# Reordering the weight loads, squares, a table load and the last mean square of a one-core hybrid decoder layer

## The chip, the cores and the metric

The kernel runs on one core of one Trainium2 chip. The metric is the device time of one execution in microseconds (us); lower is better. Engines are named as in the profile: PE is TensorE (its weight loads are PEld), DVE is VectorE, ACT is ScalarE, POOL is GpSimd, SP is SyncE, which issues most transfers. The profile is one execution taken by the hardware profiler.

## What is computed

One layer of a decoder over 1024 prompt tokens and 8 x 8 sample tokens, model width 2048, in float32. The part that the change touches is the modulation, the first norm, the start of the input projection, and the last norm:

```python
mod = jax.nn.silu(c) @ w_ada + b_ada
shift, scale, gate = jnp.split(mod[:, None, :], 3, axis=-1)
xn = rmsnorm(x, norm_g) * (1.0 + scale) + shift
z = xn @ w_in
...
out = jnp.concatenate([ya, yb, yc], axis=-1) @ w_out
return x + gate * out, new_hist_a, h_last, new_hist_b, vn
...
y = rmsnorm(x, final_g)
```

Between the two projections three token mixers work on slices of `z`: a gated linear recurrence, a convolution group of width 31, and a chunked spatial gate.

## The kernel before

Activations lie with channels on the 128 partitions and tokens along the free dimension. The tokens are worked in two parts: part 0 is the first 512 prompt tokens, part 1 the other 512 and the 64 sample tokens (576 columns, in two halves of 288). Every product of the projections is made three times (`mm3`, L130 to L133): ACT rounds a weight block to a high half (`w_hi`, L97), DVE takes the remainder (`w_lo`, L98), and PE adds hi x hi, lo x hi and hi x lo.

The stage at issue is the first one. `load_x0` (L674) loads the 16 blocks of `x0`, ACT squares them, and `var_mm` sums them on PE; `rstd_rows` (L199) makes the reciprocal root, with a Sqrt on ACT that needs a table of its own; `row_bcast` spreads it to all partitions, and L727 copies it to `R0`.

The modulation needs 2048 x 4096 weights for shift and scale. They are worked in 16 units, one for each block of 128 channels. A unit is four `ada_block`s (L708): each loads 128 x 1024 weights (512 KB, `a_raw`) and issues 8 matmuls, into 32 columns of the array each, so a unit is 32 matmuls into `ps_ada`. When the unit is done, ACT copies the result (`rows`, L177), PE turns it (`ada_turn`, L181; called the turn below), DVE makes shift and scale of it (`ada_fin`, L189 to L194: the three `adam` operations), and `norm_x` makes the normed block: DVE scales x (L243), ACT writes `xn_hi` (L244), DVE writes `xn_lo` (L245).

The main loop then takes 16 steps (L732 to L738). Step i loads unit i + 1 and issues its matmuls, makes `xn[i]`, and calls `k_step(i)` (L683), which loads block i of `w_in` (128 x 768, `w_raw`), splits it, and issues 18 matmuls of 512 columns into `ps_g`. The turn of unit i + 1 is called in the middle of `k_step(i)`. After the loop, single output blocks (`ps_s`) go on, and 64 units of the gate's modulation are put between them (`gate_block`, L152: pieces of 8 matmuls).

What sets the order in each engine's queue is not the order of the code alone. The code gives each operation a priority (`tc.high_priority`), and a scheduler of the framework puts the operations of each engine in one fixed list when the kernel is built, by priorities and by its own estimate of when data are there. On the chip each engine takes its list strictly from the front.

At the end, `out_part` (L570) works part 1's last two output blocks in two halves (L622 to L659); after each half the mean square of the finished rows is summed (`rstd_of`, L654), spread with `row_bcast`, and all 16 output blocks are scaled (L657) and stored.

Of the kernel before, what the change touches and what calls it, by code (L numbers as in the profile page):

```python
# [10 lines left out]
AF = mybir.ActivationFunctionType  # L11
ALU = mybir.AluOpType
PSUM = bass.MemoryType.PSUM

P = 128
KT = 16
EPS = 1e-6
T0 = 512
# [21 lines left out]
N_GRP = 6  # L40
# [4 lines left out]
def decoder_layer(ctx: ExitStack, tc: tile.TileContext, a):  # L45
    nc = tc.nc
# [15 lines left out]
    def mi(name):  # L62
        return pmi.tile([P, 512], F32, tag="mi", name=name)
# [12 lines left out]
    ident = cpool.tile([P, P], F32, name="ident")  # L76
    make_identity(nc, ident)
    one_d = cpool.tile([P, 1], F32, name="one_d")
# [17 lines left out]
    def split(raw, hi, lo):  # L96
        nc.scalar.copy(hi, raw)  # L97
        nc.vector.tensor_tensor(lo, raw, hi.bitcast(F32), op=ALU.subtract)  # L98

    def load_w(src, n, pieces, pool=None):  # L100
        out = []
        with tc.high_priority(HP):
            raw = wp.tile([P, 1024], F32, tag="wr", name="w_raw", bufs=3)
            nc.sync.dma_start(raw[:, :n], src)
            w = n // pieces
            for q in range(pieces):
                if pool is None:
                    hi = wp.tile([P, 512], F32R, tag="wh", name="w_hi", bufs=5)
                    lo = wp.tile([P, 512], F32R, tag="wl", name="w_lo", bufs=4)
                else:  # L110
                    hi = pool.tile([P, TM], F32R, tag="t", name="w_hi")
                    lo = pool.tile([P, TM], F32R, tag="t", name="w_lo")
                split(raw[:, q * w:(q + 1) * w], hi[:, :w], lo[:, :w])
                out.append((hi, lo))
        return out
# [19 lines left out]
    with tc.high_priority(10 * HP):  # L135
        sg = ap.tile([P, KT, 9], F32, tag="sg", name="sg", bufs=1)
        nc.gpsimd.memset(cz, 0.0)
        nc.scalar.activation(sg, cT, AF.Sigmoid)
        nc.vector.tensor_tensor(sg, sg, cT, op=ALU.mult)
        nc.vector.tensor_copy(cz[:, :, 0:9], sg)  # L140

    def ada_mm(pa, raws, b, fine):
        for q in range(2):
# [36 lines left out]
    def ada_turn(pa):  # L180
        nc.tensor.transpose(pa[:, P:2 * P], rows_of["now"], ident)  # L181
        return pa[:, P:2 * P].rearrange("p (a b) -> p a b", b=32)[:, :, 0:9]

    def ada_fin(k, pa):
        pt = ada_turn(pa)
        with tc.high_priority(HP):
            dst = adam[:, 2 * k:2 * k + 2, :]
            o = VEC["b_ada"][0] + 2 * k
            nc.vector.tensor_tensor(dst, pt[:, 0:2, :],  # L189
                                    vec[:, o:o + 2].unsqueeze(2).to_broadcast([P, 2, 9]), op=ALU.add)  # L190
            nc.vector.tensor_tensor(dst, dst, pt[:, 2:4, :], op=ALU.add)
            o = VEC["norm_g"][0] + k
            sc = adam[:, 2 * k + 1, :]
            nc.vector.tensor_scalar(sc, sc, 1.0, vec[:, o:o + 1], op0=ALU.add, op1=ALU.mult)  # L194

    def halves(T):
        return [(0, 512)] if T == T0 else [(0, 288), (288, 576)]

    def rstd_rows(src, w):  # L199
        st = stp.tile([P, 3, 144], F32, tag="st", name="st", bufs=1)  # L200
        v, r, q = st[:, 0, 0:w], st[:, 1, 0:w], st[:, 2, 0:w]
        nc.vector.tensor_scalar(v, src, EPS, None, op0=ALU.add)
        nc.scalar.activation(q, v, AF.Sqrt)
        nc.vector.reciprocal(r, q)
        nc.vector.tensor_tensor(q, r, r, op=ALU.mult)
        nc.vector.tensor_tensor(q, q, v, op=ALU.mult)
        nc.vector.tensor_scalar(q, q, -0.5, 1.5, op0=ALU.mult, op1=ALU.add)
        nc.vector.tensor_tensor(r, r, q, op=ALU.mult)
        return st

    def row_bcast(st, w, j0, n):
        pb = mi("ps_bc")
        for j in range(n):
            nc.tensor.matmul(pb[:, j * w:(j + 1) * w], ident[:, 32 * (j0 + j):32 * (j0 + j) + 1].to_broadcast([P, P]),  # L214
                             st[:, 1, 0:w], start=True, stop=True)
        return pb
# [6 lines left out]
    def rstd_of(src, u, n, ones):  # L223
        pv = mi("ps_var")
        w = n // 4
        for s in src:
            var_mm(pv, s, u, w, ones, s is src[0], s is src[-1])
        return rstd_rows(pv[:, 0:w], w)
# [341 lines left out]
    def out_part(tp, T, xd, yd, mx, sizes):  # L570
# [12 lines left out]
        acc = tp.tile([P, TM], F32, tag="t", name="acc_y")  # L583
# [38 lines left out]
        if T > T0:  # L622
            fin = []
            for d in (KT - 2, KT - 1):
                x = sp_.tile([P, TM], F32, tag="xr", name="x_r")
                nc.sync.dma_start(x[:, :T], xd[d])
                ys[d] = mp.tile([P, TM], F32, tag="mx", name=f"y{d}")
                ps = pmm.tile([P, 2, 512], F32, tag="mm", name="ps_s")
                src = a["wo_s"][d - N_GRP]
                pool = tp if d < KT - 1 else None  # L630
                fin.append((d, x, ps, load_w(src[0], 1024, 2, pool) + load_w(src[1], 1024, 2, pool)))
            for (h, (u, v)) in enumerate(halves(T)):
                for (d, x, ps, hl) in fin:
                    y = ys[d]
                    g = adam[:, 32 + d, :]
                    for k in range(KT):
                        xh, xl = xs(k)
                        hi, lo = hl[k // 4]
                        o = k % 4 * P
                        mm3(ps[:, h, :v - u], hi[:, o:o + P], lo[:, o:o + P], xh[:, u:v], xl[:, u:v],  # L640
                            k == 0, k == KT - 1)
                    with tc.high_priority(HP):
                        e = min(v, T0)
                        nc.vector.scalar_tensor_tensor(y[:, u:e], ps[:, h, 0:e - u], g[:, 0:1], x[:, u:e],
                                                       op0=ALU.mult, op1=ALU.add)
                        if v > T0:
                            y3 = y[:, T0:T1].rearrange("p (b l) -> p b l", b=8)
                            nc.vector.tensor_tensor(y3, ps[:, h, T0 - u:v - u].rearrange("p (b l) -> p b l", b=8),
                                                    g[:, 1:9].unsqueeze(2).to_broadcast([P, 8, 8]), op=ALU.mult)
                            nc.vector.tensor_tensor(y[:, T0:T1], y[:, T0:T1], x[:, T0:T1], op=ALU.add)  # L650
                        nc.scalar.activation(x[:, u:v], y[:, u:v], AF.Square)
                        nc.vector.tensor_tensor(acc[:, u:v], acc[:, u:v], x[:, u:v], op=ALU.add)
                with tc.high_priority(HP):
                    pb = row_bcast(rstd_of([acc], u, v - u, one_d), (v - u) // 4, 0, 4)  # L654
                for q in range(KT):
                    yq = ys[q]
                    nc.vector.scalar_tensor_tensor(yq[:, u:v], yq[:, u:v], vs("fg", q), pb[:, :v - u],  # L657
                                                   op0=ALU.mult, op1=ALU.mult)
                    (nc.scalar if q % 2 and h else nc.sync).dma_start(yd[q][:, u:v], yq[:, u:v])  # L659
            return  # L660
# [13 lines left out]
    def load_x0(k, pv):  # L674
        with tc.high_priority(HP):
            x = mp.tile([P, TM], F32, tag="mx", name=f"x0_{k}")
            nc.sync.dma_start(x[:, :T0], a["x0"][k])
            x0.append(x)
            sq = sp_.tile([P, TM], F32, tag="xr", name="x_sq")
            nc.scalar.activation(sq[:, :T0], x[:, :T0], AF.Square)  # L680
            var_mm(pv, sq, 0, P, one_d, k == 0, k == KT - 1)

    def k_step(k, turn):  # L683
        hl = load_w(a["wi_g"][k], N_GRP * P, 2)
        xh, xl = xn[k]
        for c in range(N_GRP):
            hi, lo = hl[c // 3]
            o = c % 3 * P
            mm_unit(gt[c // 2], c % 2, hi[:, o:o + P], lo[:, o:o + P],
                    xh, xl, T0, k == 0, k == KT - 1)  # L690
            if c == 2 and turn:
                turn()

    ada_ps = {}
# [35 lines left out]
    gt.extend(pmm.tile([P, 2, 512], F32, tag="mm", name="ps_g") for _ in range(3))  # L730
    ada_fin(0, ada_ps[0])
    for i in range(KT):  # L732
        if i + 1 < KT:
            for b in range(4):
                ada_block(i + 1, b)
        with tc.high_priority(HP):
            xn[i] = norm_x(i, x0[i], R0, T0)
        k_step(i, (lambda: ada_fin(i + 1, ada_ps[i + 1])) if i + 1 < KT else None)  # L738
    loc = [(gt[c // 2], c % 2) for c in range(N_GRP)]
    nc.sync.dma_start(bs, a["bs"])  # L740
    nc.sync.dma_start(vec[:, 64:], a["vec"][:, 64:])
# [159 lines left out]
```

## Time and profile before

| | us |
|---|---|
| median of three runs | 1527.75 (1524.29 to 1527.92) |
| the profiled execution | 1527.3 |
| its span in the trace | 1525.6 |
| PE busy | 1480.7 (97%) |
| DVE busy | 931.0 (61%) |
| ACT busy | 600.9 (39%) |
| POOL busy | 47.8 (3%) |

The span is what the trace covers; 1.7 us of the profiled execution lie around it. Busy time is the time in which an engine has at least one instruction under way. PE's matmuls are pipelined, so that a matmul that the trace shows with 0.39 us starts 0.23 us after the one before it: the pitch from start to start is what counts, not the duration.

### The profile page before, as it was taken

How to read it: one execution, taken by the hardware profiler on the slowest of the kernel's cores; microseconds unless marked ns; L12 is line 12 of the kernel's file. 1: busy time of each engine (PE TensorE's matmuls, PEld its weight loads, DVE VectorE, ACT ScalarE, POOL GpSimd, SP SyncE). 2: the span in 40 equal slices, each digit the busy share in tenths (PEclk: the TensorE clock that was granted, in tenths of full speed). 3: DMA queues.
4: the chain of work that ended last, by engine and by line, in shares of the span. 5: the costliest groups of instructions: out<-in, count | busy, mean ns of one | idle time of the engine just before them, and what ended most of it. 6: DMA issues, size and time to landing. Idle time of an engine off the chain costs nothing.

```text
span 1525.6 us, 25535 instructions
## 1 busy us (share of the span) xinstructions
PE 1480.7 (97%) x10184; PEld 1316.9 (86%) x10184; DVE 931.0 (61%) x1777; ACT 600.9 (39%) x1014; POOL 47.8 (3%) x120
## 2 busy tenths in 40 slices
PE   6999999999999999999999999999999999999996
PEld 4666788888777778888899999999999999999995
DVE  2334995498657443454895996277966754334345
ACT  4224432263547443343543422225445743322220
POOL 0000000010000000000000000010000000000000
PEclk8999999999999999999999999999999999999998
DMA  9987323333444443465473222222322222243323
GB/s 360 396 287 250 98 76 97 97 91 127 166 160 149 162 161 103 139 208 171 145 247 113 75 84 90 83 75 86 101 74 83 69 74 63 79 132 123 107 78 124
DMA packets 86550, 206.10 MB, mean 135 GB/s; under 512 B 10784, under 2 KB 26656, under 8 KB 86432
## 3 DMA queue, kind: packets, MB, share of 16 engines
q1 hardware_dynamic: 85136, 203.23, 40.6%
q8 instruction: 79, 1.29, 0.3%
q10 hardware_dynamic: 1296, 1.25, 0.3%
q14 instruction: 39, 0.32, 0.1%
HBM read 194.70 MB, written 9.74 MB: 134 GB/s over the span
## 4 chain that ended last, share of the span: by engine, by line
PE 89%; DVE 5%; DMA 3%; issue 1%; ACT 1%; SPq 0%; DVEq 0%; ACTq 0%
PE ps_s L131 22%; PE ps_s L132 22%; PE ps_s L133 22%; PE ps_g L133 6%; PE ps_g L132 5%; PE ps_g L131 5%; PE ps_ada L147 3%; DMA a_raw<-w_ada 1%; DVE w_lo L98 1%; DMA x<-x 1%; PE ps_bc L214 1%; PE ps_gate L131 1%; PE ps_gate L132 0%; DMA vec<-vec 0%; DMA w_raw<-wi_g 0%
## 5 line engine op out<-in xcount | busy, mean ns | idle before, releaser
L98 DVE TENSOR_TENSOR w_lo<-w_raw,w_hi 128x512 fp32r<-128x512 f32 (+1 forms) x480 | 311.7, 653 | 408.1 <-PE ps_s L133 269.3
L131 PE MATMUL ps_s<-xn_hi,w_hi 128*128 128x288 f32 (+1 forms) x1632 | 538.3, 330 | 1.9 <-ACT pad_a L439 1.7
L97 ACT CAST w_hi<-w_raw 128x512 fp32r<-128x512 f32 (+1 forms) x480 | 281.7, 591 | 653.4 <-PE ps_s L132 462.5
L132 PE MATMUL ps_s<-xn_lo,w_hi 128*128 128x288 f32 (+1 forms) x1632 | 534.7, 328 | 0.0
L133 PE MATMUL ps_s<-xn_hi,w_lo 128*128 128x288 f32 (+1 forms) x1632 | 532.8, 326 | 0.0
L131 PEld LDWEIGHTS ps_s<-xn_hi,w_hi 128*128 128x128 f32 x1632 | 306.1, 188 | 28.8 <-issue 2.8
L133 PEld LDWEIGHTS ps_s<-xn_hi,w_lo 128*128 128x128 f32 x1632 | 307.2, 188 | 22.2 <-issue 0.4
L132 PEld LDWEIGHTS ps_s<-xn_lo,w_hi 128*128 128x128 f32 x1632 | 306.5, 188 | 21.4 <-issue 0.9
L376 DVE SCALAR_TENSOR_TENSOR mx<-pad_b,vec,mx 128x512 f32<-128x512 f32 x240 | 178.0, 746 | 2.3
L131 PE MATMUL ps_s<-m_hi,w_hi 128*128 128x288 f32 (+1 forms) x480 | 157.2, 327 | 0.0
L132 PE MATMUL ps_s<-m_lo,w_hi 128*128 128x288 f32 (+1 forms) x480 | 156.6, 326 | 0.0
L133 PE MATMUL ps_s<-m_hi,w_lo 128*128 128x288 f32 (+1 forms) x480 | 156.5, 326 | 0.0
L133 PE MATMUL ps_g<-xn_hi,w_lo 128*128 128x288 f32 (+1 forms) x288 | 95.6, 332 | 2.3 <-DVE w_lo L98 2.2
L131 PE MATMUL ps_g<-xn_hi,w_hi 128*128 128x288 f32 (+1 forms) x288 | 96.3, 334 | 1.2
L131 PEld LDWEIGHTS ps_s<-m_hi,w_hi 128*128 128x128 f32 x480 | 90.0, 188 | 6.5 <-issue 0.2
L133 PEld LDWEIGHTS ps_s<-m_hi,w_lo 128*128 128x128 f32 x480 | 90.3, 188 | 6.1
L132 PEld LDWEIGHTS ps_s<-m_lo,w_hi 128*128 128x128 f32 x480 | 90.1, 188 | 6.3
L131 PE MATMUL ps_g<-m_hi,w_hi 128*128 128x288 f32 (+1 forms) x288 | 94.2, 328 | 0.1
L132 PE MATMUL ps_g<-xn_lo,w_hi 128*128 128x288 f32 (+1 forms) x288 | 94.3, 327 | 0.0
L132 PE MATMUL ps_g<-m_lo,w_hi 128*128 128x288 f32 (+1 forms) x288 | 93.9, 326 | 0.0
L133 PE MATMUL ps_g<-m_hi,w_lo 128*128 128x288 f32 (+1 forms) x288 | 93.6, 326 | 0.0
L133 PEld LDWEIGHTS ps_g<-xn_hi,w_lo 128*128 128x128 f32 x288 | 54.2, 188 | 12.3 <-DVE w_lo L98 8.9
(199 smaller groups left out, 1475.2 us busy)
## 6 DMA issues: line engine op xcount, KB each, us to landing
w_raw<-wi_s SPq DMA_DIRECT2D x136, 512.0 KB, 3.6
w_raw<-wo_s SPq DMA_DIRECT2D x40, 512.0 KB, 3.5
a_raw<-w_ada SPq DMA_DIRECT2D x64, 256.0 KB, 6.9
a_raw<-w_ada SPq DMA_DIRECT2D x32, 512.0 KB, 7.4
g_raw<-w_ada SPq DMA_DIRECT2D x64, 256.0 KB, 3.1
w_raw<-wi_g SPq DMA_DIRECT2D x16, 384.0 KB, 7.1
w_raw<-wo_g SPq DMA_DIRECT2D x16, 384.0 KB, 3.0
w_raw<-wi_g SPq DMA_DIRECT2D x32, 192.0 KB, 2.4
```

The source lines that it names most:

```text
L97: nc.scalar.copy(hi, raw)
L98: nc.vector.tensor_tensor(lo, raw, hi.bitcast(F32), op=ALU.subtract)
L131: nc.tensor.matmul(out, wh, xh, start=start, stop=False)
L132: nc.tensor.matmul(out, wh, xl, start=False, stop=False)
L133: nc.tensor.matmul(out, wl, xh, start=False, stop=stop)
L147: nc.tensor.matmul(pa[32 * j:32 * j + 32, 0:P], cz[:, k, :], raws[q][:, j * P:(j + 1) * P], start=(t == 0), stop=(t == (7 if fine else 15)))
L214: nc.tensor.matmul(pb[:, j * w:(j + 1) * w], ident[:, 32 * (j0 + j):32 * (j0 + j) + 1].to_broadcast([P, P]), st[:, 1, 0:w], start=True, st ...
L376: nc.vector.scalar_tensor_tensor(out[:, :T0], pad[:, j:j + T0], w[:, j:j + 1], out[:, :T0], op0=ALU.mult, op1=ALU.add)
```

## The change

Four edits:

1. The load and the split of block i of `w_in` move from the head of `k_step` to the head of the loop's step, ahead of the loads of unit i + 1.
2. A Sqrt of one column is put behind the Sigmoid at the very start, so that the root's table is loaded there.
3. Of the 16 squares of `x0`, the eight of odd k go to DVE.
4. The mean square of the last two half stages is not summed by four matmuls into 32 partitions each, with tokens along the free dimension, but by three matmuls of one column each, with 96 tokens on the partitions: the root is then worked on a tile of 96 x 3 instead of 128 x 72, and three matmuls of 96 columns spread it.

```diff
         nc.vector.tensor_copy(cz[:, :, 0:9], sg)
+        nc.scalar.activation(sg[:, 0, 0:1], one_d, AF.Sqrt)
...
-    def rstd_rows(src, w):
+    def rstd_rows(src, w, p=P):
         st = stp.tile([P, 3, 144], F32, tag="st", name="st", bufs=1)
-        v, r, q = st[:, 0, 0:w], st[:, 1, 0:w], st[:, 2, 0:w]
+        v, r, q = st[0:p, 0, 0:w], st[0:p, 1, 0:w], st[0:p, 2, 0:w]
...
-                    pb = row_bcast(rstd_of([acc], u, v - u, one_d), (v - u) // 4, 0, 4)
+                    pv, pb = mi("ps_var"), mi("ps_bc")
+                    w = 96
+                    for c in range((v - u) // w):
+                        nc.tensor.matmul(pv[0:w, c:c + 1], acc[:, u + c * w:u + (c + 1) * w], one_d,
+                                         start=True, stop=True)
+                    st = rstd_rows(pv[0:w, 0:(v - u) // w], (v - u) // w, w)
+                    for c in range((v - u) // w):
+                        nc.tensor.matmul(pb[:, c * w:(c + 1) * w], st[0:w, 1, c:c + 1].to_broadcast([w, P]),
+                                         ident[0:w, 0:w], start=True, stop=True)
...
-            nc.scalar.activation(sq[:, :T0], x[:, :T0], AF.Square)
+            if k % 2:
+                nc.vector.tensor_tensor(sq[:, :T0], x[:, :T0], x[:, :T0], op=ALU.mult)
+            else:
+                nc.scalar.activation(sq[:, :T0], x[:, :T0], AF.Square)
...
-    def k_step(k, turn):
-        hl = load_w(a["wi_g"][k], N_GRP * P, 2)
+    def k_step(k, hl, turn):
...
     for i in range(KT):
+        hl = load_w(a["wi_g"][i], N_GRP * P, 2)
         if i + 1 < KT:
             for b in range(4):
                 ada_block(i + 1, b)
         with tc.high_priority(HP):
             xn[i] = norm_x(i, x0[i], R0, T0)
-        k_step(i, (lambda: ada_fin(i + 1, ada_ps[i + 1])) if i + 1 < KT else None)
+        k_step(i, hl, (lambda: ada_fin(i + 1, ada_ps[i + 1])) if i + 1 < KT else None)
```

Because the scheduler lays the lists anew, the first edit changes the lists of PE, DVE and ACT in the main loop as well, not only SP's.

PE in the main loop before, the same in every step: from the end of one step's product through the whole of the next unit and its turn into the next step (`ps_ada<-a_raw` are a unit's matmuls, `ps_ada<-ident,rows` is the turn, `ps_g` the product).

```order
L133 MATMUL ps_g<-xn_hi,w_lo 128x512
L147 MATMUL ps_ada<-a_raw,cz 32x128 x32
L181 MATMUL ps_ada<-ident,rows 128x128
L131 MATMUL ps_g<-xn_hi,w_hi 128x512
L132 MATMUL ps_g<-xn_lo,w_hi 128x512
L131 MATMUL ps_g<-xn_hi,w_hi 128x512
L133 MATMUL ps_g<-xn_hi,w_lo 128x512
```

PE in the main loop with the change, from the turn of one unit through the start of the next step's product:

```order
L182 MATMUL ps_ada<-ident,rows 128x128
L133 MATMUL ps_g<-xn_hi,w_lo 128x512
L131 MATMUL ps_g<-xn_hi,w_hi 128x512
L132 MATMUL ps_g<-xn_lo,w_hi 128x512
L133 MATMUL ps_g<-xn_hi,w_lo 128x512
L148 MATMUL ps_ada<-a_raw,cz 32x128 x8
L131 MATMUL ps_g<-xn_hi,w_hi 128x512
L148 MATMUL ps_ada<-a_raw,cz 32x128 x8
L132 MATMUL ps_g<-xn_lo,w_hi 128x512
L148 MATMUL ps_ada<-a_raw,cz 32x128 x4
L133 MATMUL ps_g<-xn_hi,w_lo 128x512
```

The unit's 32 matmuls, one block before, now stand in four or five pieces between the matmuls of the product, and the turn, which stood ahead of all 18 product matmuls of its step, stands behind 12 to 15 of them. The steps alternate: after the turn there are four product matmuls and a piece of 8 in one step (three and a piece of 16 in the second and fourth), six and a piece of 8 in the next.

DVE in the main loop before: the three `adam` operations, the split, and the block's norm, in every step.

```order
L189 TENSOR_TENSOR adam<-ps_ada,vec 128x18
L191 TENSOR_TENSOR adam<-adam,ps_ada 128x18
L194 TENSOR_SCALAR adam<-adam,vec 128x9
L98 TENSOR_TENSOR w_lo<-w_raw,w_hi 128x384 x2
L243 SCALAR_TENSOR_TENSOR x_4_145<-x_4_145,adam,R_111 128x512
L245 SCALAR_TENSOR_TENSOR xn_lo<-x_4_145,adam,xn_hi 128x512
```

DVE in the main loop with the change, two steps, of which the first stands behind a turn with few product matmuls after it:

```order
L190 TENSOR_TENSOR adam<-ps_ada,vec 128x18
L192 TENSOR_TENSOR adam<-adam,ps_ada 128x18
L98 TENSOR_TENSOR w_lo<-w_raw,w_hi 128x384
L195 TENSOR_SCALAR adam<-adam,vec 128x9
L98 TENSOR_TENSOR w_lo<-w_raw,w_hi 128x384
L244 SCALAR_TENSOR_TENSOR x_4_146<-x_4_146,adam,R_112 128x512
L246 SCALAR_TENSOR_TENSOR xn_lo<-x_4_146,adam,xn_hi 128x512
...
L195 TENSOR_SCALAR adam<-adam,vec 128x9
L244 SCALAR_TENSOR_TENSOR x_5_154<-x_5_154,adam,R_112 128x512
L98 TENSOR_TENSOR w_lo<-w_raw,w_hi 128x384 x2
L246 SCALAR_TENSOR_TENSOR xn_lo<-x_5_154,adam,xn_hi 128x512
```

The split stands ahead of the scaling of x in one step, as before, and behind it in the other. The split is now that of the same step as the norm behind it, where before it was that of the step under way.

## Rows read from the trace of the kernel before

**Rows 1.** The page's part 4: the chain that ended last, by engine.

```profile
PE 89%; DVE 5%; DMA 3%; issue 1%; ACT 1%; SPq 0%; DVEq 0%; ACTq 0%
```

**Rows 2.** Windows: stretch, length, busy of each engine (instructions), granted PE clock, DMA share, GB/s.

```profile
60.00:80.00 20.00, 18.49 (x192) 13.38 (x196) 8.62 (x21) 4.60 (x10) 0.00 (x0) 1.00 1.04 396
100.00:120.00 20.00, 18.23 (x242) 13.60 (x240) 6.60 (x15) 4.63 (x11) 0.00 (x0) 1.00 0.64 221
```

**Rows 3.** PE's timeline, one step: start, duration (us), what, [idle before <- releaser].

```profile
36.75 0.33 PE L181 MATMUL ps_ada<-ident,rows 128*128 128x128 f32 x1 [0.44 <-ACT rows L177]
37.16 0.50 PE L131 MATMUL ps_g<-xn_hi,w_hi 128*128 128x512 f32 x1
...
38.28 0.50 PE L133 MATMUL ps_g<-xn_hi,w_lo 128*128 128x512 f32 x1 [0.16 <-DVE w_lo L98]
38.62 0.40 PE L131 MATMUL ps_g<-xn_hi,w_hi 128*128 128x512 f32 x1
...
41.63 0.39 PE L133 MATMUL ps_g<-xn_hi,w_lo 128*128 128x512 f32 x1
41.94 1.95 PE L147 MATMUL ps_ada<-a_raw,cz 128*32 128x128 f32 x64
44.34 0.33 PE L181 MATMUL ps_ada<-ident,rows 128*128 128x128 f32 x1 [0.44 <-ACT rows L177]
```

**Rows 4.** PE's timeline, one piece of the gate's modulation between products.

```profile
367.88 0.39 PE L133 MATMUL ps_s<-xn_hi,w_lo 128*128 128x512 f32 x1
368.20 0.64 PE L147 MATMUL ps_ada<-g_raw,cz 128*32 128x128 f32 x16
368.77 0.50 PE L131 MATMUL ps_s<-xn_hi,w_hi 128*128 128x512 f32 x1
369.11 0.40 PE L132 MATMUL ps_s<-xn_lo,w_hi 128*128 128x512 f32 x1
```

**Rows 5.** DVE's and ACT's timelines, the step of rows 3.

```profile
37.11 0.18 DVE L189 TENSOR_TENSOR adam<-ps_ada,vec 128x18 f32<-128x18 f32 x1 [3.77 <-PE ps_ada L181]
...
38.61 0.74 DVE L243 SCALAR_TENSOR_TENSOR x<-x,adam,R 128x512 f32<-128x512 f32 x1
40.15 0.75 DVE L245 SCALAR_TENSOR_TENSOR xn_lo<-x,adam,xn_hi 128x512 fp32r<-128x512 f32 x1 [0.79 <-ACT xn_hi L244]
...
39.39 0.72 ACT L244 ACTIVATE xn_hi<-x,adam 128x512 fp32r<-128x512 f32 x1 [1.87 <-DVE x L243]
```

**Rows 6.** PE's and ACT's timelines: first, second and last turn, first xn_hi, last product matmul.

```profile
25.59 0.47 PE L181 MATMUL ps_ada<-ident,rows 128*128 128x128 f32 x1
29.19 0.33 PE L181 MATMUL ps_ada<-ident,rows 128*128 128x128 f32 x1 [0.44 <-ACT rows L177]
...
135.17 0.33 PE L181 MATMUL ps_ada<-ident,rows 128*128 128x128 f32 x1 [0.44 <-ACT rows L177]
...
144.10 0.39 PE L133 MATMUL ps_g<-xn_hi,w_lo 128*128 128x512 f32 x1
...
27.58 0.72 ACT L244 ACTIVATE xn_hi<-x,adam 128x512 fp32r<-128x512 f32 x1 [2.04 <-DVE x L243]
```

**Rows 7.** The start: the chain that ended last, then ACT's timeline.

```profile
20.84 7.22 DMA a_raw<-w_ada
...
17.39 1.28 ACT L203 ACT_TABLE_LOAD   x1
18.69 0.31 ACT L203 ACTIVATE st<-st 128x128 f32<-128x128 f32 x1
```

**Rows 8.** The last mean square: timelines of PE and DVE.

```profile
1510.51 0.33 PE L220 MATMUL ps_var<-acc_y,one_d 128*32 128x72 f32 x8 [2.29 <-DVE acc_y L652]
...
1511.52 0.60 DVE L204 RECIPROCAL st<-st 128x72 f32<-128x72 f32 x1 [0.39 <-ACT st L203]
...
1513.31 1.95 PE L214 MATMUL ps_bc<-st,ident 128*128 128x72 f32 x8 [2.46 <-DVE st L208]
```

**Rows 9.** Windows, a stretch with waits in a later stage (columns as in rows 2).

```profile
188.00:192.00 4.00, 3.17 (x16) 2.66 (x16) 3.38 (x7) 0.41 (x1) 0.00 (x0) 0.74 0.15 43
```

## The prediction

> **What bounds the kernel now.** I read the chain that ended last first: PE holds 89% of it [rows 1], so a change counts by what it does to PE's list and to what PE waits for. Then the windows of the stage that the first edit moves: between 60 and 80 us PE is busy 18.49 of 20 us at full granted clock while the transfers run at 396 GB/s, and by 100 to 120 us they have fallen to 221 GB/s [rows 2]. Transfers were at their limit but ran ahead; PE sets the pace. Third, one step on PE's timeline: from turn to turn 44.34 - 36.75 = 7.59 us [rows 3], and over all steps (135.17 - 29.19) / 14 = 7.57 us [rows 6]. A step holds 18 product matmuls at a pitch of (41.63 - 38.62) / 13 = 0.23 us, a unit of 1.95 us in one block, a wait of 0.44 us for ACT's copy, and the turn, 0.41 us to the next matmul; the wait for `w_lo` and the changes between matmul shapes make up the rest [rows 3]. What one must see: the turn stands ahead of all 18 product matmuls, so the work behind it on DVE and ACT (shift, scale, x, `xn_hi`, `xn_lo`) has 4.8 us of PE's work to hide in. It is done 40.15 + 0.75 - 36.75 = 4.15 us after the turn [rows 3, 5], and PE never waits for it.
>
> **The change, step by step.** The sum is made against the profiled execution, 1527.3 us, 0.45 under the median of the runs; times within 0.3% (4.6 us) cannot be told from no change.
>
> *Loads ahead of the unit.* That `w_raw` comes a unit earlier on SP's queue is worth little by itself, since transfers are ahead. What counts is that PE's list is now laid differently: the unit is cut in pieces, and the turn comes late in the step.
>
> Price of a cut: one piece of 8 matmuls between products shows it. From the product matmul ahead to the one behind 368.77 - 367.88 = 0.89, and 0.34 to the next, against two pitches, 0.46: 0.77 us for the piece [rows 4]. Eight matmuls of a whole unit take 1.95 / 4 = 0.49 [rows 3], so a cut costs 0.28. The Trainium skill (TensorEngine Tiling (Array Packing), Key Properties) says that a change of tiling mode drains the array, which speaks against this change; with the 128 cycles of array depth in its TensorE: Matmul & The Clock Gate (Step-by-step), an estimate is 0.05 us for each drain, 0.11 for a cut, and the sum below would then end near 1536. I keep the measured piece. Pieces of 4 are not in the trace; I give them the same 0.28 (from 0.1, were most of it hidden, to 0.36, if each repeats a fill).
>
> The turn between products: 0.41, plus 41.94 - 41.63 - 0.23 = 0.08 going in and 0.34 - 0.23 = 0.11 coming out: 0.60 [rows 3].
>
> A step with four pieces is 18 x 0.23 + 1.95 + 4 x 0.28 + 0.60 = 7.81 us, one with five 8.09; a pair 15.90, without any wait, against 15.14 before. The 0.44 us for ACT's copy are gone (two or three product matmuls cover it), but the cuts cost more.
>
> New waits: `xn_hi` of the next block opens the next step's product, and the turn now comes late. With the split ahead of x it is ready 39.39 + 0.72 - 36.75 = 3.36 us after the turn [rows 3, 5]. PE has until then the turn (0.41), four product matmuls (0.34 + 3 x 0.23 = 1.03) and a piece of 8 (0.08 + 0.57): 2.09. It waits 1.27. In the other step x goes first: the first `xn_hi` in the trace, made so, is ready 27.58 + 0.72 - 25.59 = 2.71 us after its turn [rows 6], and six product matmuls and a piece cover 2.55: a wait of 0.16. `xn_lo` follows 0.8 later, behind more pieces, and costs nothing. A pair is 17.33 us, 2.19 more than before, and seven pairs **+15.3 us**. Bounds: 5.3 with no wait at all, 20 with cuts at 0.36 and waits 0.3 longer.
>
> Start of the loop: the split of block 0 now stands ahead of x on DVE, so the product opens at 25.59 + 3.36 = 28.95, not at 29.6, but 12 product matmuls (2.76) and 24 of the unit in four pieces (1.46 + 4 x 0.28), with 0.08 to change, come before the second turn: 34.4 against 29.19 [rows 6], **+5.2 us**. End of the loop: behind the last turn two wide splits of the next weights (0.65 each by the page's mean) stand on DVE ahead of `xn_lo`: x is ready 38.61 + 0.74 - 36.75 = 2.60 after the turn, then 1.3 and 0.75, so 4.65; 15 product matmuls follow, the last one starting 8.0 after the turn, against 144.10 - 135.17 = 8.93 before [rows 6]: **-0.9 us**. What comes behind hangs on the last product as before and moves with it as a whole; the transfers queued there wait for the same buffers.
>
> *Root table early and squares on DVE.* The table load takes 1.28 us, but was over at 18.67, when DVE's input to the root had been ready some 0.25 us [rows 7]. Squares and root then hide behind the unit's transfer of 20.84 to 28.06 on the chain [rows 7], and DVE is free there: **0**, at best -0.3. The Trainium skill (ScalarE: Activation LUTs, What ACT_TABLE_LOAD costs) counts 2.66 us with a drain for each switch; were that all on the path, the time would be 1543. The trace shows a next instruction 0.02 us behind the load.
>
> *Single columns.* Reciprocal at 72 elements takes 0.60 [rows 8]; at 3 I take 0.2. The other five small DVE operations fall from 0.23 to about the 0.18 of an 18-column one [rows 5]: 0.4 + 0.25 less. The spreading keeps 288 columns with three weight loads for four: 1.95 [rows 8], at most 0.5 less, I take 0.2. Three one-column matmuls with 96-column weights are not in the trace: from 0.1 to 1.0 (three turns of 0.33) against 0.33, I take no change. **-0.9 us**, between -1.5 and +0.3. The first half's copy of this hides behind products.
>
> Sum: 15.3 + 5.2 - 0.9 - 0.9 = +18.7, so **1546 us**.
>
> **Rivals.** *Cuts but no waits*: if `xn_hi` comes sooner, or PE is slowed so much by cuts that it finds everything ready, a pair is 15.90: 7 x 0.76 = 5.3, the start +5.2, the end -3.1, the tail -0.9: 1534. Against it speak the 3.36 us of rows 3 and 5. *Cuts nearly free*: the pieces cost their columns alone; a pair is then 2 x (4.14 + 1.95 + 0.41) = 13.0 with waits grown to about 2.0, so 15.0; with +4 at the start and -0.9 twice 1528, no change. Rows 4 speak against it. *Faster*: this mechanism with the waits gone too: the 1.07 us of a step in which PE does not stream (7.57 - 6.50) are filled by the pieces, 7 x 2.14 = 15 us less, +4, -3.1, -0.9: 1512. It decides only where a cut costs under some 0.05 us and the block is ready within 1.8 us of the turn; rows 5 say 3.36. *Clock*: in a later stage with waits the granted clock fell to a mean of 0.74, a part of the stretch at 1.2 GHz, with PE busy 3.17 of 4 us [rows 9]. Were the loop at 1.2 GHz throughout, a pair would double its 12.2 us of streaming, less the waits, some +75 us: 1621. But the new waits are 1.4 in 17.3 us, less than the idle share of now, at full clock [rows 2].
>
> **How the numbers follow.** Forecast (cuts and waits) 0.74, its own range 1538 to 1556 by the bounds above; cuts without waits 0.13; no change 0.05; faster 0.05; clock 0.03. The range of 0.8 runs from 1533, which takes in the second case, to 1556. Faster by over 0.3%: 0.05; within: 0.05; slower: 0.90.
>
> **What would show it.** Right: turns 8.6 to 8.7 us apart in the mean, alternating; 0.89 us around pieces of 8; PE waiting 1.3 us for `xn_hi` in every other step; the last product near 164 instead of 144; all later stages shifted alike; a final root under 4 us from sum to first scaling. Wrong: turns under 7.6 us apart, PE waiting for `a_raw`, or a later stage that gives the shift back.

## The result, and the profile after

| | kernel before | with the change |
|---|---|---|
| median of the runs, us | 1526.72 (4 runs) | 1546.41 (1545.47 to 1549.36, 4 runs) |
| ratio | | 1.0134, 95% interval 1.0115 to 1.0154 |
| the profiled execution / its span, us | 1527.3 / 1525.6 | 1545.47 / 1543.8 |
| first, second, last turn, us | 25.59, 29.19, 135.17 | 24.53, 35.01, 157.70 |
| start of the last product matmul of the loop, us | 144.10 | 165.36 |

The change makes the kernel slower by 1.3%; the forecast was 1546 us, its range 1533 to 1556. The lines of the changed kernel carry numbers one higher than before from L141 on (the unit's matmuls are L148, the turn L182, `xn_hi` L245).

First, one pair of steps on PE's timeline with the change, from turn to turn to turn (start, duration, what, idle before and its releaser). A record of x16 is a piece of 8 matmuls of the unit, one of x8 a piece of 4.

```profile
79.51 0.27 PE L182 MATMUL ps_ada<-ident,rows 128*128 128x128 f32 x1
...
80.64 0.65 PE L148 MATMUL ps_ada<-a_raw,cz 128*32 128x128 f32 x16
82.75 0.49 PE L131 MATMUL ps_g<-xn_hi,w_hi 128*128 128x512 f32 x1 [1.47 <-ACT xn_hi L245]
83.18 0.64 PE L148 MATMUL ps_ada<-a_raw,cz 128*32 128x128 f32 x16
83.75 0.50 PE L132 MATMUL ps_g<-xn_lo,w_hi 128*128 128x512 f32 x1
...
88.29 0.28 PE L182 MATMUL ps_ada<-ident,rows 128*128 128x128 f32 x1
...
90.86 0.96 PE L131 MATMUL ps_g<-xn_hi,w_hi 128*128 128x512 f32 x3 [0.30 <-ACT xn_hi L245]
...
93.68 0.40 PE L132 MATMUL ps_g<-xn_lo,w_hi 128*128 128x512 f32 x1
94.00 0.42 PE L148 MATMUL ps_ada<-a_raw,cz 128*32 128x128 f32 x8
94.36 0.50 PE L133 MATMUL ps_g<-xn_hi,w_lo 128*128 128x512 f32 x1
94.70 0.40 PE L132 MATMUL ps_g<-xn_lo,w_hi 128*128 128x512 f32 x1
...
96.87 0.28 PE L182 MATMUL ps_ada<-ident,rows 128*128 128x128 f32 x1
```

The pair takes 96.87 - 79.51 = 17.36 us, 8.68 a step; before, a step was 7.57 [rows 3, 6]. The steps alternate, 8.78 and 8.58, with waits of 1.47 and 0.30 us for `xn_hi`. A cut of a piece of 4 can be priced for the first time. From the product matmul ahead to the one behind are 94.36 - 93.68 = 0.68, and 0.34 to the next; less two pitches of 0.23 and the 0.24 that four matmuls take in a whole unit (1.95 / 8), 0.32 are left.

Why PE waits longer in the first step: DVE puts the split between the small operations and x.

```profile
80.12 0.55 DVE L98 TENSOR_TENSOR w_lo<-w_raw,w_hi 128x384 fp32r<-128x384 f32 x1
...
80.73 0.55 DVE L98 TENSOR_TENSOR w_lo<-w_raw,w_hi 128x384 fp32r<-128x384 f32 x1
81.19 0.75 DVE L244 SCALAR_TENSOR_TENSOR x<-x,adam,R 128x512 f32<-128x512 f32 x1
...
89.29 0.75 DVE L244 SCALAR_TENSOR_TENSOR x<-x,adam,R 128x512 f32<-128x512 f32 x1
```

From the turn at 79.51 to x is 1.68 us, from the turn at 88.29 only 1.00. PE's waits over the whole loop (24 to 170 us; total, times, longest), which before were 6.6 us for ACT's copy and 2.2 us for `w_lo`:

```profile
PE ps_g L131 <- ACT xn_hi L245: 16.3, 15, 2.5
PE ps_ada L182 <- ACT rows L178: 0.4, 1, 0.4
PE ps_g L132 <- DVE xn_lo L246: 0.2, 1, 0.2
```

Behind the loop a part comes back. The last product is 165.36 - 144.10 = 21.3 us late [rows 6], the piece of the gate's modulation that stood at 368.20 [rows 4] now stands at 387.17, 19.0 late. PE's waits between the loop and 330 us, before and then with the change, account for it: 4.6 us in five groups against 2.3 in four.

```profile
PE ps_mix L131 <- ACT tok_h L337: 1.4, 2, 0.7
PE ps_mix L133 <- DVE tok_l L338: 1.2, 2, 0.8
PE ps_mean L310 <- DVE ln_s L307: 1.1, 1, 1.1
PE ps_tr L336 <- DVE mx L357: 0.7, 1, 0.7
PE ps_var L220 <- DVE sw L758: 0.2, 1, 0.2
```

```profile
PE ps_mix L131 <- DVE mx L358: 1.0, 1, 1.0
PE ps_mix L131 <- ACT tok_h L338: 0.7, 1, 0.7
PE ps_tr L337 <- DVE mx L358: 0.4, 1, 0.4
PE ps_mix L133 <- DVE tok_l L339: 0.2, 1, 0.2
```

The end of the kernel: the last mean square (PE, DVE, PE; rows 8 are these lines before).

```profile
1529.57 0.68 PE L658 MATMUL ps_var<-one_d,acc_y 128*96 128x1 f32 x6 [2.29 <-DVE acc_y L653]
...
1530.77 0.17 DVE L205 RECIPROCAL st<-st 96x3 f32<-96x3 f32 x1 [0.33 <-ACT st L204]
...
1531.86 1.57 PE L662 MATMUL ps_bc<-ident,st 96*128 96x96 f32 x6 [1.62 <-DVE st L209]
1533.47 3.91 DVE L666 SCALAR_TENSOR_TENSOR y<-y,vec,ps_bc 128x288 f32<-128x288 f32 x9 [1.75 <-PE ps_bc L662]
```

From the start of these matmuls to the first scaling 3.90 us pass. The reciprocal fell from 0.60 to 0.17, the spreading from 1.95 to 1.57, the first sums rose from 0.33 to 0.68.

### The profile page after: what moved, and what is told of

It is laid out like the page before. It is cut to its first block, busy times and chain, and to the rows that moved or that the text cites. A ratio compares the mean times of both kernels' runs of the same rounds, so it can differ in the third digit from the quotient of the medians.

```text
span 1543.8 us, 25524 instructions
## 1 busy us (share of the span) xinstructions
PE 1497.9 (97%) x10176; PEld 1310.6 (85%) x10176; DVE 934.1 (61%) x1785; ACT 595.7 (39%) x1007; POOL 48.6 (3%) x120
## 4 chain that ended last, share of the span: by engine, by line
PE 82%; DVE 5%; ACT 1%; issue 1%; DMA 0%; DVEq 0%; ACTq 0%
PE ps_s L131 22%; PE ps_s L132 22%; PE ps_s L133 22%; PE ps_g L131 4%; PE ps_g L132 4%; PE ps_g L133 4%; PE ps_ada L148 1%; DVE w_lo L98 1%; DVE mx L377 1%; PE ps_gate L131 1%; PE ps_gate L132 0%; DVE y L666 0%; PE ps_gate L133 0%; DMA x_n<-x 0%; DVE mx L358 0%
## 5 line engine op out<-in xcount | busy, mean ns | idle before, releaser
L131 PE MATMUL ps_g<-xn_hi,w_hi 128*128 128x288 f32 (+1 forms) x288 | 95.7, 341 | 16.4 <-ACT xn_hi L245 16.3
L132 PE MATMUL ps_g<-xn_lo,w_hi 128*128 128x288 f32 (+1 forms) x288 | 98.5, 342 | 0.2 <-DVE xn_lo L246 0.2
L131 PEld LDWEIGHTS ps_g<-xn_hi,w_hi 128*128 128x128 f32 x288 | 53.9, 189 | 23.7 <-ACT xn_hi L245 20.8
```

The costliest lines, as they stand in the source:

```text
L131: nc.tensor.matmul(out, wh, xh, start=start, stop=False)
L132: nc.tensor.matmul(out, wh, xl, start=False, stop=False)
```

## The experiments

The theory: the first edit lets the scheduler lay PE's list so that the unit is cut in pieces and the turn comes late; both cost PE's time, and nothing else in the change does. The rivals: the order of the transfers is the cost; the other edits take part; one stretch at half the granted clock is the cost. All runs were timed beside the kernel before, whose medians there were 1525.6 to 1526.1 us.

| run | what | median, us | ratio to before (95% interval) | turn to turn, us |
|---|---|---|---|---|
| e1 | edit 1 alone | 1547.99 | 1.0134 (1.0118 to 1.0151) | 8.69 |
| e2 | edits 2 to 4 alone | 1524.72 | 0.9994 (0.9983 to 1.0005) | 7.57 |
| e3 | PE's order written: unit whole, turn first | 1510.46 | 0.9897 (0.9882 to 0.9912) | 6.76 |
| e4 | same, turn behind 9 product matmuls | **1504.16** | 0.9855 (0.9840 to 0.9870) | 6.36 |
| e5 | same, behind 18 | 1521.15 | 0.9968 (0.9956 to 0.9980) | 7.35 |
| e6 | same, behind 6 | 1504.69 | 0.9862 (0.9847 to 0.9877) | 6.35 |
| e7 | unit in four pieces, a step ahead | 1611.84 | 1.0561 (1.0544 to 1.0579) | starved |
| e8 | unit whole, a step ahead | 1598.88 | 1.0481 (1.0463 to 1.0498) | starved |
| e9 | e6 with the unit in 4 pieces | 1521.37 | 0.9970 (0.9960 to 0.9980) | 7.36 |
| e10 | e4 with the unit in 8 pieces | 1543.88 | 1.0120 (1.0105 to 1.0135) | 8.66 |
| e11 | e3 with the loads of before | 1522.68 | 0.9980 (0.9971 to 0.9990) | 7.52 |
| e12 | e4 with the loads of before | 1519.06 | 0.9956 (0.9941 to 0.9971) | 7.41 |

Turn to turn is the steady step, by the first and the last of a row of even steps (e4: (120.30 - 31.20) / 14), for e1 by a pair of steps (80.68 - 63.31 = 17.37).

### Which edit: e1 and e2

e1 is the kernel before with these lines alone changed; e2 is the changed kernel with them undone.

```diff
-    def k_step(k, turn):
-        hl = load_w(a["wi_g"][k], N_GRP * P, 2)
+    def k_step(k, hl, turn):
...
     for i in range(KT):
+        hl = load_w(a["wi_g"][i], N_GRP * P, 2)
```

> Only the first edit (the block of w_in loaded and split ahead of the unit) on the kernel before. Theory (the loss is PE's list that this edit brings: the unit in four or five pieces, and the turn late in the step, so that PE waits for xn_hi): all of the loss is here, and the single columns and the earlier first turn no longer soften it: 1547 to 1549 us, turns 8.7 to 8.8 us apart from the third on, PE waiting some 15 us in all for xn_hi. Rival (the other three edits took part in the loss, by the squares on DVE or the second table load): under 1543 us. Rival (half the loss is the stretch at half the granted clock that the profile of the change shows once): turns near 8.0 apart in a profile without such a stretch.

> Edits two to four alone, the loads of w_in as before. Theory: PE's list in the loop is that of before (unit whole, turn ahead of the product), turns 7.57 us apart; 0.9 us less from the single columns and up to 1.0 from the earlier first turn: 1524.5 to 1526 us. Rival (these edits cost something in the loop): above 1528 us, turns over 7.7 apart. Rival (the first turn that comes 1.06 us earlier is worth nothing at the end, because transfers set what follows): 1525.8 us, with the last product of ps_g as late as before.

Edit 1 alone gives 1547.99 us, PE waiting 15.9 us for `xn_hi`. e2's turns are 7.57 apart, and its interval allows a gain of 2.6 us or a loss of 0.8. The whole loss is edit 1's; the rivals of the other edits fall. The rival of the clock falls too, since a pair without such a stretch takes 8.69 a step and not 8.0. But the clock has a share: two steps of e1's trace (44.54 to 54.74, 98.04 to 108.31) hold a stretch at half the clock and take 10.2 and 10.3 us, where steps of their kind take 8.8, so that such a stretch costs 1.4 to 1.5 us, of 22 in all. A third lies at the start of the loop (granted clock 0.51 from 28 to 32 us and 0.64 from 32 to 36); what it costs e1 was not parted from the rest.

### PE's list or the loads: e3 and e4

Both keep PE's matmuls of the main loop in written order. e4 touches nothing else in the code of the change; e3 also calls the turn ahead of the product. The scheduler still laid DVE's and ACT's lists anew around that order: in e4 DVE scales x straight behind the three `adam` operations in all steps but the last, and the split no longer stands between.

```diff
+    def keep(ins):
+        if pin[0]:
+            tc.keep_in_program_order(ins)
...
-        nc.tensor.matmul(out, wh, xh, start=start, stop=False)
+        keep(nc.tensor.matmul(out, wh, xh, start=start, stop=False))
...
+    pin[0] = True
     for i in range(KT):
...
-        k_step(i, hl, (lambda: ada_fin(i + 1, ada_ps[i + 1])) if i + 1 < KT else None)
+        if i + 1 < KT:
+            ada_fin(i + 1, ada_ps[i + 1])
+        k_step(i, hl, None)
+    pin[0] = False
```

> All four edits, but PE's matmuls of the main loop kept in a written order: the unit whole, its turn right behind it, then the 18 product matmuls, as in the kernel before. Loads stay in the order of the change. Theory (PE's list is the cost, the order of the loads is free): turns 7.5 to 7.7 us apart, no wait for xn_hi, 1524 to 1528 us. Rival (the order of the loads is the cost: a unit's weights come later, because a block of w_in is ahead of them on SP's queue): PE waits for a_raw instead, and the time stays above 1540 us.

> As the run with the whole unit and the early turn, but the turn behind nine of the 18 product matmuls: no cut, the copy on ACT covered by nine matmuls, and nine matmuls and the next unit between the turn and the next product. Theory (both costs of a step gone, the copy's wait and the shape changes too): a step is 18 x 0.23 + 1.95 + 0.28 + 0.12 = 6.5 us, turns 6.5 apart, no wait for xn_hi, and with the end of the loop 1508 to 1513 us, faster than both. Rival (transfers become the bound: 2.49 MB a step at 397 GB/s is 6.3 us, and the blocks behind the loop are loaded later than now): the loop is quick at first, PE then waits for a_raw, or the stages after the loop wait for w_raw, and the time is 1516 to 1524 us. Rival (order of loads is the cost): above 1540 us.

The rival (the order of the loads is the cost) falls: with the loads of the change and the unit whole, the kernel is faster than before, not slower. But e3's expectation missed too, by some 14 us: the same list as before was to take the same time, and a step is 0.81 us shorter. Its timeline:

```profile
87.79 1.95 PE L154 MATMUL ps_ada<-a_raw,cz 128*32 128x128 f32 x64
90.19 0.33 PE L188 MATMUL ps_ada<-ident,rows 128*128 128x128 f32 x1 [0.44 <-ACT rows L184]
90.27 0.47 PE L137 MATMUL ps_g<-xn_hi,w_hi 128*128 128x512 f32 x1
```

The copy's 0.44 us are as in rows 3. But the product follows the turn after 0.08 us, not 0.41, and PE no longer waits for `w_lo`. What the 0.41 were is in the kernel before, in the row of PE's weight load behind a turn, and in ACT's row ahead of it (the matmul's row shows no wait, since the turn's own row lasts 0.33 of the 0.41):

```profile
90.23 0.19 PEld L131 LDWEIGHTS ps_g<-xn_hi,w_hi 128*128 128x128 f32 x1 [0.27 <-ACT w_hi L97]
...
89.66 0.93 ACT L97 CAST w_hi<-w_raw 128x384 fp32r<-128x384 f32 x2
```

ACT casts `w_hi` behind its copy of the rows, which waits for the unit, so the product waits for `w_hi`. With the load a unit earlier, ACT still casts behind its copy, but the block of the next step, and between 60 and 130 us PE's weight loads wait for neither half; before, they wait there 2.7 us for `w_hi` and 5.9 for `w_lo`.

e4 also covers the copy with nine product matmuls. Its step:

```profile
84.01 0.40 PE L139 MATMUL ps_g<-xn_hi,w_lo 128*128 128x512 f32 x1
84.34 1.95 PE L154 MATMUL ps_ada<-a_raw,cz 128*32 128x128 f32 x64
86.22 0.50 PE L137 MATMUL ps_g<-xn_hi,w_hi 128*128 128x512 f32 x1
86.56 0.39 PE L138 MATMUL ps_g<-xn_lo,w_hi 128*128 128x512 f32 x1
...
88.18 0.40 PE L139 MATMUL ps_g<-xn_hi,w_lo 128*128 128x512 f32 x1
88.41 0.27 PE L188 MATMUL ps_ada<-ident,rows 128*128 128x128 f32 x1
88.44 0.47 PE L137 MATMUL ps_g<-xn_hi,w_hi 128*128 128x512 f32 x1
88.76 0.39 PE L138 MATMUL ps_g<-xn_lo,w_hi 128*128 128x512 f32 x1
```

No wait is left. A turn between products costs 88.76 - 88.18 - 2 x 0.23 = 0.12 us, and a whole unit 86.56 - 84.01 - 2 x 0.23 = 2.09, 0.14 above its own 1.95. 18 x 0.23 + 2.09 + 0.12 = 6.35. So the code of the change, with PE's matmuls of the loop in the order in which they are written, takes 1504.16 us, and 42 us more with the lists that the scheduler made of it on its own. How much of the 42 is DVE's list was not tried apart. The transfers run at their limit meanwhile, in e4 from 60 to 90 us (busy of PE, PEld, DVE, ACT, POOL, clock, DMA share, GB/s):

```profile
60.00:90.00 30.00, 30.00 (x381) 23.87 (x374) 14.65 (x34) 8.34 (x19) 0.00 (x0) 1.00 1.04 397
```

### The price of the late turn: e5 and e6

Only the number in `if c == 2 and turn` differs from e4: 5 (behind all 18) and 1 (behind six).

> As the run with the unit whole and the turn behind nine product matmuls, but the turn behind all 18: late as in the change, and no cut. Between the turn and the next product stand only the turn and the unit, 0.12 + 2.09 = 2.2 us, and xn_hi has taken 2.5 us (x ahead of the split) to 3.2 us (split ahead) from its turn. Theory (a late turn costs its wait, apart from the cuts): PE waits 0.3 to 1.0 us for xn_hi in each step, turns 6.7 to 7.3 apart, 1508 to 1518 us. Rival (waits are made up by transfers, which are the limit at 6.3 us a step): turns stay at 6.36 to 6.45 apart and the time within 3 us of 1504.

> The turn behind six of the 18 product matmuls instead of nine, the unit whole. In the run with nine, the last step of the loop has no unit behind its turn, and PE waits there 1.1 us for xn_hi and 0.3 us for xn_lo. Theory: with 12 product matmuls (2.8 us) behind the turn that wait is gone, turns stay 6.36 apart: 1502 to 1504 us. Rival (DVE still works the next splits ahead of xn_lo there, or the stage behind the loop is bound by DVE and does not use what it is given): 1504 to 1505 us, no difference.

e5's turns are 7.35 apart and its time is 17 us above e4's, 3 above the range: 8.4 us of waits for `xn_hi` and, unforeseen, 4.0 for `xn_lo`, which in the changed kernel has pieces of the unit to hide behind (PE, 24 to 170 us).

```profile
PE ps_g L137 <- ACT xn_hi L251: 8.4, 15, 2.9
PE ps_g L138 <- DVE xn_lo L252: 4.0, 14, 0.3
```

The wait for `xn_hi` in e6's last step is gone, its last product starts 1.7 us before e4's (126.63 against 128.36), and its time is e4's: what is behind the loop gave it back. The rival was right.

### The price of a cut: e7 to e10

e7 and e8 worked the unit a step ahead, e7 in four pieces between the products, e8 whole.

```diff
     for i in range(KT):
         hl = load_w(a["wi_g"][i], N_GRP * P, 2)
         if i + 1 < KT:
             with tc.high_priority(HP):
-                xn[i] = norm_x(i, x0[i], R0, T0)
+                xn[i + 1] = norm_x(i + 1, x0[i + 1], R0, T0)
...
+            if turn and c < 4:
+                ada_block(turn, c)
```

> Cuts without waits: the unit is worked one step further ahead (unit i + 2 in step i), in four pieces of eight between the product matmuls, its turn behind 15 of them, and the block of x is normed a whole step before its product, so that PE has nothing to wait for. Theory (a cut costs about 0.28 us each, whether or not PE waits): a step is 18 x 0.23 + 4 x 0.77 + 0.12 = 7.3 us against 6.4 in the run with the same order and the unit whole, 14 steps, 11 to 15 us more than that run, at 1515 to 1522 us. Rival (pieces cost only their columns, the loss of the change is all waits): a step of 6.4 us, within 3 us of that run. Rival (a cut costs more than priced and the waits hide a part of it): a step of 7.6 and more.

> The partner of the run with cuts and no waits: the unit one step further ahead as there, the turn behind 15 product matmuls as there, but the unit whole. Theory: a step of 6.36 us as with the turn in the middle, no wait for xn_hi although the turn is late in its step; in the first steps PE waits for a_raw, since one more unit (5.3 us of transfers) is wanted before the second product: 1502 to 1508 us. Rival (a late turn costs something besides the wait for xn_hi): a step of over 6.6 us.

Both missed by some 90 us and tell nothing of cuts, though they lie 13 us apart as expected: the scheduler laid SP's list anew too. A unit's two wide blocks now stand first there, then the block of `w_in`, then the four narrow loads, of which PE wants the first two first. In e8, from 60 to 120 us, SP's queue waits for buffers:

```profile
SPq L721 <- PE ps_ada L154: 25.7, 10, 4.4
SPq L104 <- DVE w_lo L98: 18.5, 4, 5.1
```

The wide blocks wait for the matmuls of an earlier unit, everything behind them waits with them, and PE then waits for `a_raw`, 48.9 us between 24 and 170 us. A list of SP's in another order was not tried with these two.

e9 and e10 leave loads and norms alone. The unit's matmuls are put between the single product matmuls at the head of a step, in four pieces (turn behind six) and in eight (turn behind nine).

```diff
+            gaps.extend((i + 1, raws, p, 4) for p in range(4))
+            unit_part(*gaps.pop(0))
...
         keep(nc.tensor.matmul(out, wh, xh, start=start, stop=False))
+        if gaps:
+            unit_part(*gaps.pop(0))
```

> Cuts without waits, second attempt, which leaves the loads and the norm of x where they are: the run with the turn behind six product matmuls, and the unit in four pieces of eight with one product matmul between two of them, all ahead of the turn. 12 product matmuls and a piece stand between the turn and the next product, so nothing is to be waited for. Theory (a cut costs about what rows 4 gave): a piece of eight takes 0.77 us between products, so a step is 18 x 0.23 + 4 x 0.77 + 0.12 = 7.34 us against 6.36 with the unit whole, 15 steps, +14.9 us: 1518 to 1521 us. Rival (a piece costs its columns and the 0.05 for each drain of the notes' estimate): 0.33 us a step, +5 us, 1509 to 1511 us. Rival (cuts free): 1504 to 1506 us.

> Twice the cuts: the unit in eight pieces of four, one product matmul between two of them, the turn behind nine product matmuls. Nine product matmuls and a piece (2.6 us) stand between the turn and the next product, about what xn_hi takes (2.5 us), so that a wait of up to 0.1 us a step may be left. Theory: a piece of four takes 0.55 us between products, as read in the profile of the change (0.31 above its columns), so a step is 18 x 0.23 + 8 x 0.55 + 0.12 = 8.66 us, 2.3 more than whole: 1536 to 1541 us. Rival (the price falls when the piece is small): a step under 8.0 us, below 1530 us.

Steps of 7.36 and 8.66 us, as priced. Three more pieces cost 7.36 - 6.35 = 1.01, 0.34 each, seven more 8.66 - 6.36 = 2.30, 0.33 each, in steps without waits. In e10 one product matmul and one piece of 4 repeat every 0.78 us (94.61 - 93.83), 0.31 above 0.23 and 0.24:

```profile
93.83 0.49 PE L137 MATMUL ps_g<-xn_hi,w_hi 128*128 128x512 f32 x1
94.25 0.43 PE L736 MATMUL ps_ada<-a_raw,cz 128*32 128x128 f32 x8
94.61 0.49 PE L140 MATMUL ps_g<-xn_lo,w_hi 128*128 128x512 f32 x1
```

e10's time is 2.9 us above its range although its steps are as expected: the first two (25.61 to 47.88, with a wait of 2.3 us and a stretch at half the clock) take 5.0 us more than two later ones. e9 is 0.4 above its range.

### What the early load is worth: e11 and e12

e3 and e4 with the load and split of `w_in` back in `k_step`, as in the kernel before.

```diff
     for i in range(KT):
-        hl = load_w(a["wi_g"][i], N_GRP * P, 2)
...
-    def k_step(k, hl, turn):
+    def k_step(k, turn):
+        hl = load_w(a["wi_g"][k], N_GRP * P, 2)
```

> The run with the unit whole and the turn ahead of all product matmuls in written order, but the block of w_in loaded and split behind the unit, as in the kernel before. It parts the order of the loads from the written order of PE: that run took 6.76 us a step against 7.57 of the kernel before. Theory (the 0.8 us come from the split, which the earlier load lets ACT and DVE work a step ahead, so that w_hi and w_lo are there when the turn is done): a step is 7.5 to 7.9 us again, PE waiting for w_lo, 1522 to 1530 us. Rival (the 0.8 us come from the order of the products that was written out): 6.76 us a step, 1509 to 1512 us.

> The run with the unit whole and the turn behind nine product matmuls, but the block of w_in loaded and split behind the unit, as in the kernel before. DVE's list then has the split of a block ahead of the next turn's work. Theory (with the turn out of the way the split is early enough wherever its load stands): turns 6.36 to 6.5 us apart, 1504 to 1507 us, and the first edit would not be needed. Rival (the load is too late behind the unit, since transfers are at their limit of 6.3 us a step): PE waits for w_hi or w_lo in each step, over 6.7 us a step, 1509 us and more.

| step, us | loads of before | loads of the change |
|---|---|---|
| turn first | 7.52 (e11) | 6.76 (e3) |
| turn behind nine | 7.41 (e12) | 6.36 (e4) |

The early load is worth 0.76 us a step in one row and 1.05 in the other. e11 came as its theory said (7.52, 1522.68 us): between 60 and 130 us the weight loads wait again, 2.7 us for `w_hi` and 5.1 for `w_lo`, where in e3 they wait for neither. In e12 the rival's numbers came, but not by its reason: PE waits for `w_hi` although the turn is out of the way, and `w_hi` waits for ACT and not for a transfer (PE and ACT in e12):

```profile
87.51 0.50 PE L137 MATMUL ps_g<-xn_hi,w_hi 128*128 128x512 f32 x1 [0.85 <-ACT w_hi L97]
...
86.78 0.27 ACT L184 COPY rows<-ps_ada 128x128 f32<-128x128 f32 x1 [1.86 <-PE ps_ada L154]
86.94 0.93 ACT L97 CAST w_hi<-w_raw 128x384 fp32r<-128x384 f32 x2
```

The cast stands behind the copy of the rows on ACT. My theory there (the split is early enough) looked at DVE's list and not at ACT's.

## Why the prediction was right, and where not

By its own terms, in us:

| term | predicted | measured |
|---|---|---|
| start of the loop, up to the second turn | +5.2 | 35.01 - 29.19 = +5.8 |
| 14 steps between second and last turn | +15.3 | 122.69 - 105.98 = +16.7 |
| last turn to last product | -0.9 | 7.66 - 8.93 = -1.3 |
| behind the loop | 0 | 19.0 - 21.3 = -2.3 |
| last mean square, from its sums' start to the scaling | -0.9 | 3.90 - 4.79 = -0.9 |
| sum | +18.7 | +18.0 (of the spans: 1543.8 - 1525.6 = +18.2) |

*The pair of steps*: 17.33 predicted, 17.36 in the trace. The mechanism (cuts, a late turn, waits for `xn_hi` that alternate) is what the trace shows, but that the size agrees to 0.03 is luck: errors of 0.96 and 1.00 made each other up. **The turn between products** was put at 0.60 us and takes 0.12. The failed step is that "the turn, 0.41 us to the next matmul" was read as the turn's own cost; e3, with the loads of the change, shows that it is a wait for `w_hi`, hidden in a row of PE's weight load and not in the matmul's. That is 0.96 too much in a pair. Too little were the pieces (five in each steady step, not four and five in turn, and 0.32 for one of 4 instead of 0.28) and the waits (1.47 + 0.30 instead of 1.27 + 0.16); and the first product matmul behind a wait takes 0.11 longer to the next start, as one behind a piece does (82.75 to the piece at 83.18 is 0.43, where 93.68 to 94.00 is 0.32), twice in a pair. That is 0.28 + 4 x 0.04 + 0.34 + 0.22 = 1.00.

*The other terms* made each other up as well. Up to the second turn +5.8 against +5.2: the first turn came 1.06 us earlier, which was not in the sum, but from first to second turn passed 35.01 - 24.53 = 10.48 us and not the 34.4 - 25.59 = 8.8 of the sum. PE had idled 2.51 us for `xn_hi` up to 28.03, and the granted clock then was 0.57 for 4 us, which lost PE some 4 x 0.43 = 1.7 us, an estimate:

```profile
28.00:32.00 4.00, 3.97 (x29) 1.98 (x29) 0.75 (x1) 0.00 (x0) 0.00 (x0) 0.57 1.04 398
```

In the 14 steps (+16.7 against +15.3) a stretch at half the clock took 1.5 (below), and behind the loop 2.3 came back. The bounds of the sum do not fit each other: nine cuts at 0.36 and two waits 0.3 longer are 9 x 0.08 + 0.6 = 1.32 a pair, 24.6 in seven and not 20, and no waits at all end at 1536 and not at 1538.

*Cuts*: 0.28 by rows 4, 0.33 and 0.34 measured by e9 and e10. The estimate from the Trainium skill (TensorEngine Tiling (Array Packing), Key Properties, and TensorE: Matmul & The Clock Gate, Step-by-step) was 0.11 for a cut; that changes of mode cost something agrees with the runs, the size of that estimate does not. The rivals in which cuts are nearly free, or fill idle time, fall with that; cuts without waits falls with the 16.3 us of waits.

*Waits*: e5 shows that a turn as late as this costs 0.99 us a step without any cut, e9 and e10 that cuts cost without any wait. In the changed kernel a step of 8.68 is e4's 6.36, four more pieces (4 x 0.33 = 1.32) and waits of 0.89 in the mean, 8.57; the 0.11 left are as much as the slower start behind a wait. So of the 2.3 us between e4 and the change, cuts are the larger part, 1.3. The size of the waits hangs on DVE's list too (1.68 and 1.00 us from the turn to x, above), and no run changed that list alone.

*"Worth little by itself"*: this sentence on the early load was wrong. It looked at the transfers, which were ahead, and not at ACT's and DVE's lists, in which the split moves a step forward. By e11 and e12 it is worth 0.76 to 1.05 us a step. The prediction did not suffer, since the pair was summed from PE's work without any of the waits of before; but the reason why the kernel got slower is not that the edit is worthless. The edit's gain was more than taken back by the list that came with it.

*"Moves with it as a whole"*: 2.3 us come back behind the loop, and the waits shown above shrink by as much. Why they shrink was not tried.

*Clock*: the rival's extreme (the loop at 1.2 GHz throughout) did not come; the windows from 90 to 180 us have a granted clock of 1.00. Two stretches near half the clock are in the loop, that at its start (28 to 32 us, above) and one in a later step (66 to 68 us, at 1.2 GHz):

```profile
66.00:68.00 2.00, 2.00 (x11) 0.93 (x12) 0.00 (x0) 0.00 (x0) 0.00 (x0) 0.50 0.95 305
```

The step that holds it takes 70.95 - 60.69 = 10.26, 1.5 more than others of its kind (8.78). PE had waited 1.68 us some 2 us earlier; other waits of 1.5 us in the loop are not followed by such a stretch. Together the two cost some 3 of the 18 us in this trace, the one at the start by the estimate above. The prediction's sum has neither.

*Table and squares*: the first turn comes 1.06 us earlier (24.53), more than the 0.3 allowed, but e2 cannot tell edits 2 to 4 from no change. The table load takes 1.28 us from 5.06 on, and ACT's next instruction begins at 6.35; of the 2.66 us that the Trainium skill (ScalarE: Activation LUTs, What ACT_TABLE_LOAD costs) counts for a switch, the load agrees, and the drain does not show here either. *Single columns*: as forecast in sum, though the parts differ: the sums took 0.68 where no change from 0.33 was taken, and the spreading fell by 0.38 where 0.2 was taken.

## What to carry to other kernels

When an edit moves a load, read what it does to each engine's list before its own merit: here the lists cost 36 to 42 us against the same code with PE's matmuls in a written order (1546.41 against 1510.46 and 1504.16). Keep a block of matmuls of another shape whole, and put a short dependent step (the turn) in the middle of long independent work, with enough ahead of it for its input and behind it for its users. A wait for weights can be missing from the matmul's row and stand only in the weight load's (the 0.27 us above); a gap behind a small matmul is not that matmul's cost until those rows have been read.

## What the runs showed that was not expected

- By the spans of the two traces e4 gains 1525.6 - 1502.2 = 23.4 us, but only 144.10 - 128.36 = 15.7 at the end of the loop. Behind it PE's waits up to the first gate product are 1.1 us instead of 4.6, and the last mean square gives 0.9. The 3.3 left are about what a stretch at half the clock costs that the kernel before has from 190 to 196 us (6 us at 0.50, an estimate of at most 3) and that does not occur in e4's trace. The clock's part rests on one trace each.
- Where PE was starved the granted clock fell over long stretches. In e7 from 90 to 120 us PE was busy 19.68 of 30 us and the clock's mean 0.77, between its two levels of 1.2 and 2.4 GHz; the changed kernel, busy 26.44 us in the same window, had 1.00.

```profile
90.00:120.00 30.00, 19.68 (x166) 11.55 (x166) 6.22 (x14) 4.02 (x8) 0.00 (x0) 0.77 0.53 167
```
